# Attention by pairs of heads in plain fp32, on halves of the TensorE array, in a two-layer hybrid decoder

## The chip, the core and the metric

The kernel runs on one core of one Trainium2 chip. The metric is device time in microseconds (us) from launch to end; lower is better. The engines are TensorE (PE in the profile, PEld for its weight loads), VectorE (DVE), ScalarE (ACT), GpSimd (POOL) and SyncE (SP), which here issues most DMAs.

## The reference

Two layers over 512 tokens of width 1024. Each layer first mixes the tokens by three groups that read slices of one input projection, then runs a gated feed-forward net (FFN) of width 2816 with a short convolution. All data are float32.

```python
for l in range(DEPTH):
    h = rms_norm(x, attn_norm[l])
    (q_a, k_c, v_c, k_s, v_s, k_w, v_w, gate_a,
     c_q, c_kv, k_r, u) = jnp.split(h @ w_in[l], split_points, axis=-1)
    o_a = nsa_attention(...)
    o_b = mla_attention(...)
    o_c = s5_ssm(...)
    mix = jnp.concatenate([rms_norm(o_a, ...), rms_norm(o_b, ...), rms_norm(o_c, ...)], axis=-1)
    x = x + mix @ w_out[l]
    x = x + conv_ffn(rms_norm(x, ffn_norm[l]), ...)
return rms_norm(x, final_norm)
```

The two attention groups have six heads each. In the first, "NSA", a head has 64 query columns, three heads share one key and value head, and each head is attended three times: over 31 compressed blocks, over selected blocks (with 512 tokens all of them are selected, so this is plain causal attention) and over a window (again causal). The three results are added with gates. In the second, "MLA", a head has 96 query columns (64 plus 32 rotary ones), and one causal attention. So a layer has 6 x 2 + 6 = 18 causal attentions of 512 x 512 with 64 value columns.

## The kernel before, in words

**Numbers.** TensorE takes a float32 operand in two ways here. Plain `F32` is the ordinary one. `F32R` is a rounded form. The kernel gets float32 accuracy from the rounded form by splitting an operand into a rounded high part and a remainder: `split` writes the high part with ACT and the remainder with DVE or POOL. A product is then two or three matmuls, high x high, high x low, low x high (`mm3`, L239 to L242). Nearly all matmuls of the kernel are of this kind; each works on the full 128 x 128 array.

**A head.** One head is one unit (MLA) or two (NSA: selected, window). A unit has four stages. Stage 0 prepares operands. For NSA, `prep` stacks the high part of the 64 query rows on their remainder, 128 rows in all, and the high key part twice (L1038 to L1056), so that two matmuls of 128 rows make the scores. For MLA, `proj_q` projects 128 query rows (L928 to L943) and the scores are three matmuls. Stage 1, `head_scores` (L511), makes four blocks of scores, 128, 256, 384 and 512 columns wide, because the attention is causal; DVE adds the mask and takes the row minimum (L520), ACT takes the exponential with the row sum (L523). Stage 2, `head_scale` (L526), multiplies by the reciprocal sum and the gate on POOL (L532). Stage 3, `head_pv` (L539), does for each of four key blocks j: 4 - j transposes of 128 x 128 on PE (L544), a split of the transposed block from PSUM (ACT the high part, DVE the remainder, L546), and two matmuls (L548). Their weights are the high and the low value part side by side, 64 + 64 columns, so the head's result is the sum of two halves of the output, which `out_evac` (L570) adds with ACT and DVE. For NSA, two more matmuls (L1076) add the compressed attention.

**Order.** `pipeline` (L554) runs the units with the stages shifted by one unit each, in the order 2, 1, 3, 0. The other work of the mixer (projections, the state-space group, norms, the first part of the output projection) hangs on steps of this pipeline by the tables `PLAN0` and `PLAN1`, one for each layer. The framework then schedules the instructions with its own estimate of times, so what stands on an engine is not the order of the source; each engine runs its instructions in the order that results.

**Memory.** PSUM's eight banks are dealt out by name: two for projections ("mm", "kq"), two for scores ("s"), two for transposes ("t"), one for the result of a head ("o"), and one for everything small ("x"). SBUF has 128 x 512 tiles `f` (float32) and pairs of such tiles `r` (rounded: high and low).

**Norms.** `rstd_` (L248) computes a norm's factors for 512 tokens as 4 columns and spreads each over 128 rows by a matmul with the identity (L271).

## Time and profile before

| | |
|---|---|
| median of 3 runs | 1374.46 us (1372.62 to 1374.56) |
| span of the profiled execution (first to last instruction) | 1372.3 us |
| PE, PEld busy share of the span | 95%, 79% |
| DVE, ACT, POOL busy share | 62%, 47%, 53% |
| PE in the chain that ended last | 72% |

The profile has no end-to-end time of its own execution beside the span; the median run is 2.2 us longer than that span, so a change of the span is taken as a change of the time. In the tables of the profile, "bank" is a PSUM bank, "wt" a weight tile after its split, "raw" one before it, "sml" a small column tile, "cst" the constants (mask, identity). A plain fp32 matmul of the program stands in the trace as two MATMUL records; an F32R matmul and a transpose stand as one. Busy time of PE overlaps between neighbours, since a matmul's record reaches from its start to the end of its pipeline.

### The profile page before, as it was taken

What the parts mean: (1) busy time and instruction counts of PE and PEld (TensorE: products, weight loads), DVE (VectorE), ACT (ScalarE), POOL (GpSimd) and SP (SyncE); (2) the same over time, 40 slices, a digit from 0 to 9 for tenths busy, and PEclk for the clock granted to TensorE, in tenths of its full rate; (3) what the DMA queues carried; (4) which work ended last, traced back from release to release, by engine and by line L of the source; (5) the groups of instructions that cost most, each with busy time, mean ns of one, the idle gap of its engine ahead of it and who ended that gap; (6) DMA issues with size and microseconds to landing.
All of it is one profiled execution on the core that took longest, in us unless ns stands there. A gap on an engine that the chain in (4) does not pass through costs nothing.

```text
span 1372.3 us, 19205 instructions
## 1 busy us (share of the span) xinstructions
PE 1302.4 (95%) x6414; PEld 1079.2 (79%) x6414; DVE 856.5 (62%) x1733; ACT 638.8 (47%) x1322; POOL 724.4 (53%) x722
## 2 busy tenths in 40 slices
PE   7888989998998999999999999999999999999997
PEld 5676777786876888888888887877878888888886
DVE  6988889858695334643466488986764433442455
ACT  4334667754443233423443356886453323332344
POOL 7485546654759155545437665556376315612532
PEclk9989999999999999999999999999999999999998
DMA  6243622212333333443353433121223333333332
GB/s 224 83 131 99 182 85 66 68 62 64 98 99 113 111 95 100 117 124 95 112 173 112 149 124 106 59 60 43 83 85 106 95 100 99 94 92 106 95 94 83
DMA packets 91556, 140.14 MB, mean 102 GB/s; under 512 B 15553, under 2 KB 36545, under 8 KB 91457
## 3 DMA queue, kind: packets, MB, share of 16 engines
q1 hardware_dynamic: 90176, 134.72, 32.2%
q0 software_dynamic: 1280, 4.20, 1.0%
q8 instruction: 50, 0.82, 0.3%
q14 instruction: 50, 0.40, 0.1%
HBM read 125.01 MB, written 15.96 MB: 103 GB/s over the span
## 4 chain that ended last, share of the span: by engine, by line
PE 72%; DVE 19%; issue 3%; POOL 2%; ACT 2%; DMA 2%; SPq 0%; DVEq 0%; POOLq 0%; ACTq 0%
PE bank L240 21%; PE bank L241 20%; PE bank L242 20%; DVE r L227 3%; PE bank L519 2%; PE bank L548 2%; DVE f L520 2%; PE bank L544 2%; DVE r L230 1%; DVE f L304 1%; DVE f L1157 1%; PE bank L271 1%; PE bank L816 1%; PE bank L253 1%; POOL wt L227 1%
## 5 line engine op out<-in xcount | busy, mean ns | idle before, releaser
L240 PE MATMUL bank<-r,wt 128*128 128x512 f32 x1466 | 580.9, 397 | 15.2 <-ACT wt L226 7.3
L241 PE MATMUL bank<-r,wt 128*128 128x512 f32 x1466 | 577.0, 394 | 4.4 <-DVE r L230 3.6
L242 PE MATMUL bank<-r,wt 128*128 128x512 f32 x1466 | 573.4, 394 | 5.1 <-POOL wt L227 5.1
L227 POOL TENSOR_TENSOR wt<-raw,wt 128x512 fp32r<-128x512 f32 (+2 forms) x272 | 355.0, 1309 | 300.1 <-ACT wt L226 291.0
L226 ACT CAST wt<-raw 128x512 fp32r<-128x512 f32 (+2 forms) x398 | 231.0, 584 | 332.5 <-PE bank L241 189.6
L240 PEld LDWEIGHTS bank<-r,wt 128*128 128x128 f32 x1466 | 278.2, 190 | 77.2 <-ACT wt L226 8.9
L242 PEld LDWEIGHTS bank<-r,wt 128*128 128x128 f32 x1466 | 278.0, 190 | 66.1 <-POOL wt L227 8.5
L241 PEld LDWEIGHTS bank<-r,wt 128*128 128x128 f32 x1466 | 278.4, 190 | 62.8 <-DVE r L230 6.5
L227 DVE TENSOR_TENSOR wt<-raw,wt 128x512 fp32r<-128x512 f32 (+3 forms) x126 | 88.9, 709 | 51.7 <-ACT wt L226 51.3
L294 POOL TENSOR_TENSOR f<-f,f 128x512 f32<-128x512 f32 (+1 forms) x53 | 68.0, 1284 | 99.9 <-ACT f L286 98.4
L532 POOL TENSOR_SCALAR f<-f,sml 128x128 f32<-128x128 f32 (+3 forms) x144 | 79.3, 569 | 52.2 <-DVE sml L530 18.0
L227 DVE TENSOR_TENSOR r<-bank,r 128x256 fp32r<-128x256 f32 (+4 forms) x196 | 90.2, 476 | 24.2 <-ACT r L226 23.0
L1182 DVE TENSOR_TENSOR f<-bank,f 128x512 f32<-128x512 f32 x44 | 30.3, 690 | 112.6 <-PE bank L242 103.1
L1188 POOL TENSOR_TENSOR f<-f,f 128x512 f32<-128x512 f32 x44 | 58.0, 1320 | 74.6 <-ACT f L1187 74.6
L523 ACT ACTIVATE f<-f,sml 128x384 f32<-128x384 f32 (+3 forms) x144 | 80.6, 560 | 32.5 <-DVE sml L520 31.6
L226 ACT CAST r<-bank 128x256 fp32r<-128x256 f32 (+4 forms) x196 | 79.0, 417 | 31.8 <-PE bank L544 15.7
L548 PE MATMUL bank<-r,r 128*128 128x512 f32 (+3 forms) x288 | 82.1, 353 | 10.4 <-DVE r L227 7.5
L519 PE MATMUL bank<-r,r 128*128 128x128 f32 (+3 forms) x336 | 79.3, 339 | 9.8 <-DVE sml L520 9.5
L226 ACT CAST r<-f 128x512 fp32r<-128x512 f32 (+1 forms) x76 | 46.9, 620 | 80.5 <-DVE f L1189 65.7
L520 DVE CUSTOM_DVE_ANT_0 f<-bank,cst 128x384 f32<-128x384 f32 (+3 forms) x144 | 67.8, 481 | 12.7 <-PE bank L519 11.6
L1189 DVE TENSOR_TENSOR f<-bank,f 128x512 f32<-128x512 f32 x44 | 30.4, 690 | 72.7 <-POOL f L1188 68.9
L1217 DVE TENSOR_TENSOR f<-bank,f 128x512 f32<-128x512 f32 x48 | 32.7, 688 | 65.6 <-PE bank L242 65.5
(225 smaller groups left out, 1549.9 us busy)
## 6 DMA issues: line engine op xcount, KB each, us to landing
raw<-in_wup_dram SPq DMA_DIRECT2D x176, 256.0 KB
raw<-in_wdn_dram SPq DMA_DIRECT2D x72, 256.0 KB
raw<-in_win_dram SPq DMA_DIRECT2D x64, 256.0 KB
f<-pd SPq DMA_DIRECT2D x32, 256.0 KB
raw<-in_wout_dram SPq DMA_DIRECT2D x32, 192.0 KB
f<-in_xT_dram SPq DMA_DIRECT2D x16, 256.0 KB
f<-in_w_dram SPq DMA_DIRECT2D x16, 256.0 KB
pd<-f SPq DMA_DIRECT2D x16, 256.0 KB
```

The source lines that it names most:

```text
L226: A.copy(hi, src)
L227: (E or V).tensor_tensor(lo, src, f32(hi), op=OP.subtract)
L240: PE.matmul(p, lhsT=w[:, 0, o:o + n], rhs=x[:, 0], start=start, stop=False)
L241: PE.matmul(p, lhsT=w[:, 0, o:o + n], rhs=x[:, 1], start=False, stop=False)
L242: PE.matmul(p, lhsT=w[:, 1, o:o + n], rhs=x[:, 0], start=False, stop=stop)
L294: G.tensor_tensor(a, a, q, op=OP.add)
L519: PE.matmul(p[:, :w], lhsT=q[:, i * 128:w], rhs=k[:, :w], start=n == 0, stop=n == len(passes) - 1)
L520: V.tensor_tensor_reduce(out=sm[i], in0=p[:, :w], in1=C("mask")[:, 512 - w:], op0=OP.add, op1=OP.min, scale=1.0, scalar=3.0e38, accum_out= ...
L523: A.activation(sm[i], sm[i], AF.Exp, bias=mx[:, i:i + 1], scale=-1.0, accum_out=su[:, i:i + 1])
L532: G.tensor_scalar(sm[i], sm[i], rs[:, i:i + 1], 1.0, op0=OP.mult, op1=OP.mult)
L548: PE.matmul(o[:, j * 128:], lhsT=v[j], rhs=pr[:, x, :w], start=first and j == 0 and x == 0, stop=last and j == 3 and x == 1)
L1188: G.tensor_tensor(t, t, r_f, op=OP.mult)
```

## The change

Two heads make one unit, nothing in attention is split any more, and its operands are plain fp32.

- **Scores** (`pair_scores`). NSA: the two heads' queries lie in rows 0 to 63 and 64 to 127 of one tile, their keys likewise, and each head's block is one matmul of 64 rows, on the upper or the lower half of the array, into a bank of its own. The heads are permuted on the host so that head m and head m + 3 share a tile. MLA: one matmul of 128 rows for each head and block, on the full array.
- **Values** (`pair_pv`). The transposed blocks are copied from PSUM once (in turn by ACT and DVE, `pcopy="AVAVA"`, five copies of 512 columns for a pair) and used whole. Each head's matmul has 64 weight columns: one head writes rows 0 to 63 of the result, the other rows 64 to 127. The result is copied once by ACT; `out_evac` is gone. The compressed attention (L1061 of the changed kernel) is one such matmul for each head.
- **Operands.** Keys, values and rotary parts are copied instead of split; `prep` of NSA is empty.
- **Norm factors** are spread by `PE.transpose` instead of a matmul with the identity.
- **Banks.** "s" has three banks and takes what "x" had; "t" two, "o" one.
- **Plan.** There are nine units for each layer instead of 18, and the steps of the tables are about halved.

```diff
-CFG = dict(plan=(PLAN0, PLAN1), F=dict(main=15, aux=10, side=12), R=dict(main=16, side=3, q=3, pr=2), nraw=3, nw=4, hp=50,
-           order=(2, 1, 3, 0), rings=dict(), tabs=2, lead=(0, 0, 3, 4), units=('NNNNNNMMMMMM', 'NNNNNNMMMMMM'), rest=((-7, -1, -1, -5, -7, -1, -1, -1), (-1, -1, -3, -1, -1, -1, -1, -1)),
+CFG = dict(plan=(PLAN0, PLAN1), F=dict(main=24, aux=10, side=12), R=dict(main=16, side=3), nraw=3, nw=4, hp=50,
+           order=(2, 1, 3, 0), rings=dict(), tabs=2, lead=(0, 0, 3, 4), units=('NNNMMM', 'NNNMMM'), pcopy="AVAVA", rest=((-7, -1, -1, -5, -7, -1, -1, -1), (-1, -1, -3, -1, -1, -1, -1, -1)),
...
-    rings = dict(kq=banks[0:2], mm=banks[0:2], s=banks[2:4], t=banks[4:6], o=banks[6:7], x=banks[7:8], up=banks[0:4], dn=banks[4:8], w2=banks[0:4] + banks[6:8] + banks[2:4])
+    rings = dict(kq=banks[0:2], mm=banks[0:2], s=banks[2:5], t=banks[5:7], o=banks[7:8], up=banks[0:4], dn=banks[4:8], w2=banks[0:4] + banks[6:8] + banks[2:4])
...
     def ps(kind):
+        kind = "s" if kind == "x" else kind
...
-            PE.matmul(p[:, i * 128:(i + 1) * 128], lhsT=y[:, i:i + 1].to_broadcast([128, 128]), rhs=ident, start=True, stop=True)
+            PE.transpose(p[:, i * 128:(i + 1) * 128], y[:, i:i + 1].to_broadcast([128, 128]), ident)
...
-    def head_scores(passes):
-            p = ps("s")
-            for n, (q, k) in enumerate(passes):
-                PE.matmul(p[:, :w], lhsT=q[:, i * 128:w], rhs=k[:, :w], start=n == 0, stop=n == len(passes) - 1)
+    def pair_scores(qk):
+            p = [ps("s"), ps("s")]
+            for x, (q, k) in enumerate(qk):
+                PE.matmul(p[x][:, :w], lhsT=q[:, i * 128:w], rhs=k[:, :w], start=True, stop=True)
...
-    def head_pv(o, b, sm, v, first, last):
-            pr = R.get("pr")
-            split(p[:, :w], pr[:, 0, :w], pr[:, 1, :w])
-            for x in range(2):
-                PE.matmul(o[:, j * 128:], lhsT=v[j], rhs=pr[:, x, :w], start=first and j == 0 and x == 0,
-                          stop=last and j == 3 and x == 1)
+    def pair_pv(o, b, sm, v, first, last):
+        for k, js in enumerate(((0,), (1, 3), (2,))):
+            for n, part in enumerate(todo):
+                p, c = ps("t"), 0
...
+                if cfg["pcopy"][2 * k + n] == "A":
+                    A.copy(t, p)
+                else:
+                    V.tensor_copy(t, p)
...
+            for j in js:
+                for x in range(2):
+                    PE.matmul(o[64 * x:64 * x + 64, j * 128:], lhsT=v(x, j), rhs=pt[x, j], start=first and j == 0, stop=last and j == 2)
...
-    def out_evac(o, dst):
-        t = F.get()
-        A.copy(t[0:64], o[64:128])
-        V.tensor_tensor(dst, o[0:64], t[0:64], op=OP.add)
-        F.free(t)
...
-                for r in range(6):
-                    V.scalar_tensor_tensor(hrep[:, r, 0:31], a[:, c], 1.0, hy[:, c], op0=OP.add, op1=OP.mult)
+                V.scalar_tensor_tensor(hy, a, 1.0, hy, op0=OP.add, op1=OP.mult)
+                for kv2 in range(2):
+                    V.tensor_copy(shp(hr, 4, 2, 32)[:, 0:3, kv2, 0:31],
+                                  hy[:, kv2 * 31:kv2 * 31 + 31][:, None, :].to_broadcast([128, 3, 31]))
...
             def scores():
-                qs, K = qsl[h][:, 0], KS[g, bi]
-                st["s"] = head_scores([(qs, K[:, 0]), (qs, K[:, 1])])
+                q, k = pj[f"q{m}"], pj[("ks", "kw")[bi]]
+                st["s"] = pair_scores([(q[r:r + 64], k[r:r + 64]) for r in (0, 64)])
```

What the scheduler makes of it is seen on PE. The first place is in the second layer, among the NSA units. Before, PE's stream there reads as follows (L519: a score matmul, x2 two of them back to back; L544: a transpose; L548: a value matmul; L500 is the state-space group, L780 MLA's values):

```order
L519 MATMUL bank3_154<-r4_104,r19_119 128x512 x2
L500 MATMUL bank7_158<-f30_93,f29_92 128x64
L548 MATMUL bank6_157<-r22_122,r5_105 128x512
L780 MATMUL bank0_151<-wt3_130,r0_100 128x384
L780 MATMUL bank1_152<-wt3_130,r0_100 128x384
L548 MATMUL bank6_157<-r22_122,r5_105 128x512
L548 MATMUL bank6_157<-r23_123,r5_105 128x384
L544 MATMUL bank4_155<-cst_159,f5_68 128x128
L544 MATMUL bank4_155<-cst_159,f8_71 128x128
```

In the changed kernel the same stretch reads so (L527: a score matmul on a row half; L576: a value matmul on a column half; L564: a transpose on the full array):

```order
L527 MATMUL bank3_158<-f0_63,f6_69 128x128
L576 MATMUL bank7_162<-f16_79,f33_96 64x384
L576 MATMUL bank7_162<-f11_74,f33_96 64x128
L576 MATMUL bank7_162<-f16_79,f33_96 64x128
L564 MATMUL bank5_160<-cst_163,f28_91 128x128
L564 MATMUL bank5_160<-cst_163,f12_75 128x128
L564 MATMUL bank5_160<-cst_163,f28_91 128x128
L564 MATMUL bank5_160<-cst_163,f29_92 128x128
L527 MATMUL bank3_158<-f0_63,f6_69 128x384
L564 MATMUL bank5_160<-cst_163,f12_75 128x128
L564 MATMUL bank5_160<-cst_163,f28_91 128x128
L564 MATMUL bank5_160<-cst_163,f29_92 128x128 x2
```

Two matmuls of the same 128-row form have become matmuls of single halves, and the partners of a score pair are apart: between one half's matmul and the next stand transposes or value matmuls of another form.

The second place is DVE, also in the second layer's NSA units. Before, it reads so (L227: the remainder of a split, here of a transposed block; L520: mask and minimum of a score block, an ISA row and one that reads its minimum; L479 to L490: the state-space group):

```order
L227 TENSOR_TENSOR r22_122<-bank5_156,r22_122 128x512
L488 TENSOR_TENSOR f31_94<-f31_94 128x256
L227 TENSOR_TENSOR r23_123<-bank4_155,r23_123 128x384
L490 SCALAR_TENSOR_TENSOR f32_95<-r81_3524,f31_94 128x64 x4
L520 ISA f8_71,sml12_143<-bank2_153,cst_159 128x384
L520 ISA sml12_143 128x1
L479 TENSOR_TENSOR f31_94<-f32_95,f27_90 64x4x63 x2
L520 ISA f10_73,sml12_143<-bank3_154,cst_159 128x512
L520 ISA sml12_143 128x1
```

Afterwards (L529: mask and minimum; L570: DVE's copy of a transposed bank; L713, L228, L893 and L231: projections, a weight split, and the state-space group's output):

```order
L529 ISA f23_86,sml2_137<-bank3_158,cst_163 128x384
L529 ISA sml2_137 128x1
L570 COPY f5_68<-bank5_160 128x512
L893 SCALAR_TENSOR_TENSOR f35_98<-f38_101,f35_98 128x512
L539 RECIPROCAL sml8_143<-sml3_138 128x8
L541 TENSOR_TENSOR sml8_143<-sml8_143,gates_171 128x8
L228 TENSOR_TENSOR wt2_133<-raw1_129,wt2_133 128x384
L713 TENSOR_TENSOR f10_73<-bank1_156,f11_74 128x512
L231 SCALAR_TENSOR_TENSOR r17_126<-f35_98,r17_126 128x512
L529 ISA f8_71,sml9_144<-bank2_157,cst_163 128x512
```

The remainders of transposed blocks are gone from DVE, and two of a pair's five plain copies stand there instead.

## Rows read from the trace of the kernel before

**Rows 1.** Page, chain that ended last, by engine.
```profile
PE 72%; DVE 19%; issue 3%; POOL 2%; ACT 2%; DMA 2%; SPq 0%; DVEq 0%; POOLq 0%; ACTq 0%
```
**Rows 2.** Windows: busy time (x instructions) of each engine, granted clock, by stage.
```profile
core 0: us, PE busy (x) PEld busy (x) DVE busy (x) ACT busy (x) POOL busy (x), PEclk, DMA share, GB/s
0.00:105.00 105.00, 84.94 (x385) 69.08 (x386) 88.32 (x162) 40.48 (x68) 73.79 (x82) 0.93 0.45 145
105.00:313.00 208.00, 190.20 (x1084) 157.96 (x1083) 164.78 (x464) 132.77 (x347) 115.17 (x151) 0.96 0.30 93
...
361.00:719.00 358.00, 352.22 (x1587) 287.84 (x1586) 186.33 (x264) 137.91 (x228) 186.00 (x160) 1.00 0.37 111
...
777.00:965.00 188.00, 177.65 (x1034) 150.57 (x1034) 153.26 (x444) 130.41 (x341) 111.79 (x143) 1.00 0.26 82
```
**Rows 3.** PE timeline, full-array and 16-column matmuls: start us, us, engine line.
```profile
578.44 0.39 PE L240 MATMUL bank<-r,wt 128*128 128x512 f32 x1
578.67 0.39 PE L241 MATMUL bank<-r,wt 128*128 128x512 f32 x1
578.99 0.21 PE L447 MATMUL bank<-f 128*16 128x16 f32 x2
579.05 0.35 PE L448 MATMUL bank<-f,f 128*16 128x112 f32 x2
...
579.78 0.35 PE L448 MATMUL bank<-f,f 128*16 128x112 f32 x2
580.06 0.50 PE L240 MATMUL bank<-r,wt 128*128 128x512 f32 x1
580.40 0.40 PE L241 MATMUL bank<-r,wt 128*128 128x512 f32 x1
```
**Rows 4.** PE timeline: four transposes; the spreading of one norm's factors (eight records).
```profile
568.84 0.60 PE L440 MATMUL bank<-cst,f 128*128 128x128 f32 x4
...
1016.11 1.05 PE L271 MATMUL bank<-cst,sml 128*128 128x128 f32 x8
```
**Rows 5.** Groups by form of PE, 777 to 965 us: busy us, mean ns, idle before.
```profile
L240 PE MATMUL bank<-r,wt 128*128 128x512 f32 x106 | 42.9, 406 | 0.2 <-DVE r L227 0.2
...
L544 PE MATMUL bank<-cst,f 128*128 128x128 f32 x180 | 31.5, 274 | 1.0 <-DVE r L227 1.0
...
L843 PE MATMUL bank<-f,f 128*128 128x64 f32 x4 | 0.6, 260 | 0.0
```
**Rows 6.** Waits of PE's weight loads, 777 to 965 us: total us, times, longest.
```profile
PEld bank L548 <- DVE r L227: 9.5, 13, 1.5
PEld bank L519 <- DVE sml L520: 2.5, 4, 1.2
```
**Rows 7.** Page, groups of the heads' matmuls, whole kernel.
```profile
L548 PE MATMUL bank<-r,r 128*128 128x512 f32 (+3 forms) x288 | 82.1, 353 | 10.4 <-DVE r L227 7.5
L519 PE MATMUL bank<-r,r 128*128 128x128 f32 (+3 forms) x336 | 79.3, 339 | 9.8 <-DVE sml L520 9.5
```
**Rows 8.** PE timeline, one plain fp32 matmul of 512 columns (two records).
```profile
896.20 1.02 PE L764 MATMUL bank<-f,cst 128*128 128x512 f32 x2
```
**Rows 9.** Groups by form of DVE, 777 to 965 us.
```profile
L227 DVE TENSOR_TENSOR r<-bank,r 128x512 fp32r<-128x512 f32 x20 | 13.7, 686 | 5.2 <-ACT r L226 5.1
...
L227 DVE TENSOR_TENSOR r<-bank,r 128x128 fp32r<-128x128 f32 x30 | 8.0, 280 | 2.1 <-ACT r L226 2.1
L573 DVE TENSOR_TENSOR f<-bank,f 64x512 f32<-64x512 f32 x11 | 7.5, 682 | 1.1 <-ACT f L572 0.9
```
**Rows 10.** Chain that ended last, first layer's start: start us, us, what.
```profile
68.26 1.66 DVE r L1055
...
94.41 3.95 DVE f L841 x6
...
103.54 2.71 DVE f L850 x5
...
128.50 3.78 DVE r L1055
```

More of the change, by code (lines that the diff above doesn't have):

```diff
@@ L768, in k_rope @@
                 r0 = 64 if b == 0 else 0
-                KF.append(R.get())
-                split(p[r0:r0 + 64], KF[b][r0:r0 + 64, 0], KF[b][r0:r0 + 64, 1])
+                KF.append(F.get())
+                A.copy(KF[b][r0:r0 + 64], p[r0:r0 + 64])
         def mla_v():
             uv = wload(wuv[l], 384)
-            mv.extend(R.get() for _ in range(3))
+            mv.extend(F.get() for _ in range(4))
             for i in range(4):
@@ L956, in pv @@
-                if b == 0:
-                    ob.append(F.get())
-                out_evac(o, ob[m][64 * b:64 * b + 64])
-                if b == 1 and late == "M":
+                pair_pv(o, *st["s"][:2], lambda x, j: mv[j][:, (2 * m + x) * 64:(2 * m + x) * 64 + 64], True, True)
+                t = F.get()
+                A.copy(t, o)
+                ob.append(t)
+                if late == "M":
                     join(ob[m], 3 + m)
@@ L1019, in nsa_v @@
                 PE.transpose(p[:, i * 128:(i + 1) * 128], pj[n][:, i * 128:(i + 1) * 128], ident)
-            p4 = shp(p, 4, 2, 64)
-            for g in range(2):
-                v = vsv(g)[:, bi]
-                split(p4[:, :, g, :], v[:, :, 0, :], v[:, :, 1, :])
+            vs[bi] = F.get()
+            A.copy(vs[bi], p)
             F.free(pj[n])
-        def vsv(g):
-            return vs[g][:, :, :].rearrange("p s (i x d) -> p s i x d", i=4, x=2)
         oa = []
-        KS, qsl, ops = {}, {}, {}
@@ L1069, in pv @@
             def pv():
                 if bi == 0:
-                    ops[h] = ps("o")
-                head_pv(ops[h], *st["s"][:2], [vsv(g)[:, bi, j].rearrange("p x d -> p (x d)") for j in range(4)],
-                        bi == 0, False)
+                    ops[m] = ps("o")
+                pair_pv(ops[m], *st["s"][:2], lambda x, j: vs[bi][:, j * 128 + x * 64:j * 128 + x * 64 + 64], bi == 0, False)
                 if bi == 1:
                     for x in range(2):
-                        PE.matmul(ops[h], lhsT=vc[:, h].rearrange("p a b -> p (a b)"), rhs=pct[h // 4][:, x],
-                                  start=False, stop=x == 1)
-                    if b == 0:
-                        oa.append(F.get())
-                    out_evac(ops[h], oa[m][q0:q0 + 64])
-                    if b == 1 and late == "N":
+                        h = 2 * m + x
+                        PE.matmul(ops[m][64 * x:64 * x + 64], lhsT=vc[:, h], rhs=pct[h // 4], start=False, stop=True)
+                    t = F.get()
+                    A.copy(t, ops[m])
+                    oa.append(t)
+                    if late == "N":
@@ L1136, in tile_trunk @@
                 end.setdefault(t, []).append(tasks[n])
-        heads = dict(N=iter([[nsa_unit(h, bi) for bi in range(2)] for h in range(6)]),
-                     M=iter([[mla_unit(m, b)] for m in range(3) for b in range(2)]))
+        heads = dict(N=iter([[nsa_unit(m, bi) for bi in range(2)] for m in range(3)]),
+                     M=iter([[mla_unit(m)] for m in range(3)]))
         pipeline([u for g in order for u in next(heads[g])], mid, end)
@@ L1288, in _lay @@
     put("cvb2", a["nsa_cv_b2"][None])
[L1289 removed]
+    put("gateb", a["nsa_gate_b"][None][:, :, gp])
     put("are", np.concatenate([a["ssm_a_re"].transpose(2, 0, 1)] * 2, 0))
```

196 lines of the change are left out of this document (92 added, 104 removed), and 12 rows, old and new, of tables (PLAN0, PLAN1).

## The prediction

> **What bounds the kernel now.** I read the chain by engine first: 72% of it is PE and 19% DVE [rows 1]. So PE sets the time where it has enough work, and DVE some of the rest. Then the windows [rows 2]. In the FFN (361 to 719 us) PE is busy 352 of 358 us, and the change touches nothing there. The attention heads lie in 105 to 313 us (first layer) and 777 to 965 us (second): 208 + 188 = 396 us, with PE busy 190.2 and 177.7. Only 28 us are idle, but busy time counts the pipeline behind every matmul that had to wait. What PE must issue comes from start-to-start times. Neighbouring 512-column F32R matmuls start 0.23 us apart (578.44, 578.67), though one lasts 0.39 [rows 3]; I use 0.227, which is 0.443 ns a column. Four transposes span 0.60 us, the last of them 0.27 long, so 0.11 each [rows 4, 5]. With such prices the 26 forms of the second window, 1034 records [rows 2, 5], need about 166 us of its 188, and the first window also about 166 of 208. **PE has 332 us of own work in 396 us; 64 us are gaps.** Where they come from is in the waits: the longest total before PE's weight loads is for the remainders of split blocks (DVE L227), 9.5 us, then the masked scores, 2.5 us [rows 6]. DVE is busy 165 of 208 and 153 of 188 us there, ACT 133 and 130 [rows 2]. So the heads are bound by PE, with gaps that DVE causes.
>
> **The change part by part.**
>
> *Heads' matmuls on PE.* Gone are the 336 score and 288 value matmuls [rows 7] and 24 for the compressed part, 648 F32R matmuls with 211,968 columns by the code's widths (128 to 512): 211,968 x 0.443 ns = 94 us. New ones are plain fp32. Such a matmul of 512 columns is two records that span 1.02 us [rows 8]. An F32R matmul lasts 0.39 us and holds the array for 0.227 [rows 3], so 0.16 of a span is pipeline behind the work; the two records hold the array for 0.86 us, 0.43 each, nearly four times F32R's. That is 1.67 ns a column. MLA's scores go from three F32R matmuls to one plain one on the full array: 15,360 columns, 25.6 us. The half-array matmuls (96 scores, 156 values, 82,944 columns) cost 138 us if each runs alone. That is 138 + 25.6 - 94 = **+70 us with no overlap**. If every partner ran wholly beside its twin, they would cost 69, and the term would be +1.
>
> Between these bounds the trace has no row, since no matmul of the kernel works on a half beside another. What can overlap I take from the order: matmuls issue in order, so a half runs beside its twin only if they are neighbours. Of the 252 half-array matmuls, 107 stand directly behind one of the other half (85 value matmuls, 22 scores) with 29,824 columns; the scheduler has put transposes or projections between the others, as the two PE pieces of the order show. Each plain matmul is two passes long in two records, A, A', B, B'; of a lone pair A' can run beside B, which saves one record of four. 29,824 x 0.83 ns = 25 us. I take **+45 us**.
>
> *Norm factors.* 60 matmuls (eight records spanning 1.05 us for four of them [rows 4], about 0.11 a record) become transposes of 0.11: **-7 us**.
>
> *Changes of form.* The 16-column matmuls of the state-space group show what it costs when the array goes from one form to another [rows 3]. L241 starts at 578.67 and holds the array for 0.227; the next, of 16 columns, could start at 578.90 and starts at 578.99. On the way back L448's last record starts at about 579.87 (the second of two that start 0.095 apart) and ends its streaming by 579.97; L240 starts at 580.06, and its successor 0.34 later instead of 0.23, as its weights could not be loaded ahead. So about 0.1 us in and 0.2 back before an F32R matmul; before a transpose the same reading gives 0.15. The built order has 16 such changes before, 279 after: 263 more. At 0.145 each, **+38 us**; the bounds are nothing, where PE waits at that moment anyway, and 0.2 each, 53 us.
>
> The trace shows this for a form of 16 columns alone [rows 3]. The Trainium skill ("TensorEngine Tiling (Array Packing)", Key Properties) says that switching between tiling modes, not between tiles of one mode, drains TensorE. By it the halves pay as the 16 columns do, +38; if only the narrow form paid, 0. No run here shows it for halves.
>
> *PE in all:* 45 - 7 + 38 = +76 us.
>
> *DVE, ACT, POOL.* A head's four remainders take DVE 0.69, 0.55, 0.41 and 0.28 us, 1.93 in all (the two between lie on the line of the first and last [rows 9]); 36 heads, 69 us. `out_evac`: 24 x 0.68 = 16 us [rows 9]. New on DVE are 36 copies of 512 columns; at 0.69, the price of the nearest DVE read of a bank [rows 9], 25 us. Net about -60 us of the 318 that DVE is busy in the heads, and ACT and POOL lose some work too. This shortens nothing by itself; it takes gaps out of PE. The waits for L227 go altogether, those for masked scores stay. No DMA is moved.
>
> *Start of the first layer.* There PE has 85 us of work in 105, DVE 88 [rows 2], and the chain runs through instructions that the change takes away or merges: L1055 (1.7 and 3.8 us, stretched), six L841 (4.0), five L850 (2.7) [rows 10]. Of these 12 us perhaps 4 come back as the new copies and products: **-8 us**. What is late next is DVE's state-space work on the same chain.
>
> *Sum.* PE then has 332 + 76 = 408 us of own work for what took 396. So even with no gap left the heads are 12 us longer. Of 64 us of gaps I keep 24: the waits on split blocks go, DVE has a fifth less to do, and PE, now the later one, finds operands ready more often; but masked scores, the fill and the end of a pipeline with units twice as large stay. 408 + 24 - 396 - 8 = +28. The profiled span and the median run are taken to move alike: 1374.5 + 28 = **1402 us**. With no gap left it is 1378; with all 64 left, 1442.
>
> **The rivals.**
>
> *The halves do not overlap at all.* Nothing in the trace shows that they do. Then +70 in place of +45: 1427 us.
>
> *New waits keep the gaps.* "s" has three banks for pairs and for all that used "x", so a score block can wait for a norm or a state-space block, and POOL and ACT take a pair in blocks twice as large. For it speaks that PE's score matmuls wait for DVE already [rows 7]; against it, that DVE loses a fifth of its work. All gaps left: 1442 us.
>
> *Faster: changes of form cost nothing.* If halves switch without a drain, or nearly all changes fall where PE waits for an operand (gaps of 64 us are enough room for 38), PE has 370 us, with 24 of gaps 394, and the start 8 less: 1364 us. It decides from about 0.04 us a change on: 263 x (0.145 - 0.04) is the forecast's 28. Against it: the narrow form pays in the middle of a stream where the neighbours wait for nothing [rows 3].
>
> *Faster: pairs overlap wholly.* For this a half must run beside a twin that stands apart in the order, or all four records of a pair must overlap. Then +1 in place of +45, with the changes of form still paid: 1358 us. The Trainium skill ("TensorEngine Tiling (Array Packing)", Theoretical Speedup) gives up to 2x for a dimension of 64 or less; by it alone the pairs cost this.
>
> **How the numbers follow.** A measurement of this kernel tells 0.2%, 2.7 us, from no change. Chances: the forecast with its own range of 1385 to 1418 us 0.45, no overlap 0.2, gaps kept 0.12, the two faster rivals together 0.19, no change 0.04. So slower 0.77, same 0.04, faster 0.19. The range reaches to the middle of the faster rivals below and to the gaps kept above: 1361 to 1440 us.
>
> **What would show it.** Right, if in the profile after the two score records of a half stand 0.43 us apart at 512 columns, and a change of form leaves 0.09 to 0.2 us between the end of one matmul's streaming and the next; if the heads are longer than 208 and 188 us with PE busier, DVE's busy time falls by some 60 us, and the FFN keeps 358 us. The start would reach the first score matmul some us earlier. Wrong, if neighbours of one form start closer than one record's 0.43 us at many places and the heads are shorter; if PE shows long idle times before L527 with DVE or bank waits behind them (then the banks rule, not PE's work); or if the granted clock of the heads, 0.96 and 1.00 [rows 2], falls, for which I have no term.

## The result, and the profile after

The changed kernel takes 1470.78 us (median of 4 runs, 1470.67 to 1472.54) against 1373.54 for the kernel before beside it: 1.0711 times as long, 95% interval 1.0696 to 1.0726. It is slower, as forecast, but by 97 us in place of 28, and outside the range of 1361 to 1440. The chain that ended last has 78% PE and 11% DVE (72% and 19% in [rows 1]): DVE is off the path to a good part, and PE more than fills its place:

```profile
PE 78%; DVE 11%; POOL 3%; DMA 3%; issue 3%; ACT 1%; SPq 0%; POOLq 0%; DVEq 0%; ACTq 0%
```

Windows of the changed kernel, with the columns of [rows 2]: the start in two pieces, the first layer's heads, FFN and start of the second layer, the second layer's heads.

```profile
0.00:105.00 105.00, 72.95 (x311) 57.78 (x312) 76.36 (x150) 31.50 (x54) 58.21 (x73) 0.85 0.43 137
105.00:131.00 26.00, 25.71 (x156) 20.39 (x154) 14.43 (x30) 8.53 (x16) 17.13 (x21) 1.00 0.49 147
131.00:367.00 236.00, 218.70 (x948) 134.42 (x946) 109.40 (x315) 106.37 (x263) 96.31 (x129) 0.91 0.22 68
416.00:777.00 361.00, 351.86 (x1588) 286.73 (x1587) 187.43 (x264) 137.82 (x229) 186.02 (x160) 1.00 0.38 111
845.00:1063.00 218.00, 206.55 (x947) 128.71 (x945) 107.27 (x315) 105.51 (x261) 94.45 (x127) 0.96 0.22 65
```

The heads take 236 + 218 us in place of 208 + 188 [rows 2]: +58, where the forecast had +36 (+76 of work, 40 of gaps gone). In the first 105 us PE did 311 instructions in place of 385, and the first score comes at 131 us, 26 later; the forecast had it 8 earlier. The granted clock of these 105 us fell too, from 0.93 [rows 2] to 0.85; the lost 0.08 of 105 us is 8 us, the most that it can have cost of the 26. The rest stands before the second layer's heads: from the end of the first layer's to the first score of the second's are 479 us instead of 464, partly work that only changes its place (between the last norm and that score PE has 287 records in 55 us; before, 236 in 44).

So the start is the largest surprise. The longest waits of PE in it, first of the changed kernel (30 to 131 us), then of the kernel before (30 to 105 us): total us, times, longest.

```profile
PE bank L847 <- DVE f L846: 9.8, 1, 9.8
PE bank L241 <- DVE f L713: 4.7, 1, 4.7
PE bank L441 <- DVE f L713: 3.3, 1, 3.3
PE bank L241 <- DVE bd L851: 2.3, 1, 2.3
```

```profile
PE bank L829 <- DVE f L828: 3.6, 1, 3.6
PE bank L816 <- DMA f<-in_w_dram: 2.9, 1, 2.9
PE bank L816 <- DVE bd L834: 2.3, 1, 2.3
```

L847 of after is L829 of before: the compression's second matmul, which needs DVE's GELU. PE's timeline at this place, first after, then before (start us, us, engine, line):

```profile
45.14 3.81 PE L834 MATMUL bank<-f,f 128*128 128x62 f32 x32
58.71 0.69 PE L847 MATMUL bank<-f 128*128 128x62 f32 x2 [9.76 <-DVE f L846]
61.67 0.80 PE L241 MATMUL bank<-r,wt 128*128 128x512 f32 x1 [2.28 <-DVE bd L851]
```

```profile
45.54 3.81 PE L816 MATMUL bank<-f,f 128*128 128x62 f32 x32
49.10 0.48 PE L241 MATMUL bank<-r,wt 128*128 128x512 f32 x1
49.42 0.39 PE L242 MATMUL bank<-r,wt 128*128 128x512 f32 x1
```

Before, projections follow the compression at once, 0.23 us apart, and cover DVE's GELU. After, PE stands 9.8 us and then 2.3 more. What the small blocks had was bank 7, alone; now they take turns in "s", banks 2 to 4, and "up", the ring of these projections, is banks 0 to 3. So a small block can hold a bank that a projection needs; the wait of L241 for L851, which reads the compression's result out of its bank, is of this kind. The experiments test whether that is the cause.

In the heads the halves look like this. PE's timeline in the second layer: L576 and L1061 are column halves, L527 a score matmul (the first row a pair on row halves), L564 transposes, L243 the F32R projection before a lone half; x4 at L1061 is two matmuls of two records each.

```profile
973.07 0.49 PE L527 MATMUL bank<-f,f 64*128 64x128 f32 x4
...
985.66 0.65 PE L576 MATMUL bank<-f,f 128*64 128x256 f32 x4
986.14 1.03 PE L1061 MATMUL bank<-f,vc 128*64 128x512 f32 x4
987.10 0.66 PE L564 MATMUL bank<-cst,f 128*128 128x128 f32 x4
...
1004.99 0.39 PE L243 MATMUL bank<-r,wt 128*128 128x512 f32 x1
1005.31 0.86 PE L576 MATMUL bank<-f,f 128*64 128x384 f32 x2
1006.10 0.66 PE L564 MATMUL bank<-cst,f 128*128 128x128 f32 x4
```

Two neighbouring matmuls of 512 columns on opposite halves span 1.03 us together, what one spans alone on the full array, 1.02 [rows 8]. Each record of one runs beside the same record of the other, so a lone pair saves half of its time, not the quarter of the forecast. Row halves do the same: the pair of 128 columns spans 0.49 us, and a lone half of 128 columns 0.48 (at 219.91 us in the last fence). Yet the heads are longer than forecast. The experiments separate what overlap gives from what the halves cost.

### The profile page after: what moved, and what is told of

Its sections match the earlier page's. It is cut to its first block, busy times and chain, and to the rows that moved or that the text cites. A ratio compares the mean times of both kernels' runs of the same rounds, so it can differ in the third digit from the quotient of the medians.

```text
span 1470.8 us, 18403 instructions
## 1 busy us (share of the span) xinstructions
PE 1382.0 (94%) x6306; PEld 1048.2 (71%) x6306; DVE 752.8 (51%) x1475; ACT 584.7 (40%) x1158; POOL 690.2 (47%) x702
## 4 chain that ended last, share of the span: by engine, by line
PE 78%; DVE 11%; POOL 3%; DMA 3%; issue 3%; ACT 1%; SPq 0%; POOLq 0%; DVEq 0%; ACTq 0%
PE bank L241 20%; PE bank L243 20%; PE bank L242 20%; PE bank L527 6%; PE bank L576 5%; PE bank L564 3%; DVE r L231 1%; PE bank L254 1%; POOL wt L228 1%; DVE f L305 1%; DMA f<-pd 1%; DVE f L1141 1%; PE bank L834 1%; DVE f L529 1%; POOL f L426 0%
## 5 line engine op out<-in xcount | busy, mean ns | idle before, releaser
L241 PE MATMUL bank<-r,wt 128*128 128x512 f32 x1466 | 586.6, 401 | 29.8 <-ACT wt L227 6.8
L243 PE MATMUL bank<-r,wt 128*128 128x512 f32 x1466 | 575.8, 396 | 8.6 <-POOL wt L228 7.9
L228 POOL TENSOR_TENSOR wt<-raw,wt 128x512 fp32r<-128x512 f32 (+2 forms) x272 | 352.4, 1300 | 340.1 <-ACT wt L227 335.5
L227 ACT CAST wt<-raw 128x512 fp32r<-128x512 f32 (+2 forms) x398 | 231.2, 585 | 414.8 <-PE bank L242 236.3
L241 PEld LDWEIGHTS bank<-r,wt 128*128 128x128 f32 x1466 | 279.3, 191 | 106.8 <-issue 10.8
L243 PEld LDWEIGHTS bank<-r,wt 128*128 128x128 f32 x1466 | 279.1, 190 | 74.3 <-POOL wt L228 12.2
L228 DVE TENSOR_TENSOR wt<-raw,wt 128x512 fp32r<-128x512 f32 (+3 forms) x126 | 88.8, 708 | 62.5 <-ACT wt L227 62.2
L527 PE MATMUL bank<-f,f 64*128 64x256 f32 (+7 forms) x288 | 105.7, 506 | 6.7 <-DVE sml L529 4.3
L544 POOL TENSOR_SCALAR f<-f,sml 128x128 f32<-128x128 f32 (+3 forms) x144 | 76.1, 549 | 75.3 <-DVE sml L541 38.4
L529 DVE CUSTOM_DVE_ANT_0 f<-bank,cst 128x512 f32<-128x512 f32 (+3 forms) x144 | 68.8, 489 | 81.5 <-PE bank L527 74.8
L534 ACT ACTIVATE f<-f,sml 128x512 f32<-128x512 f32 (+3 forms) x144 | 80.4, 559 | 70.3 <-DVE sml L529 64.2
L1166 DVE TENSOR_TENSOR f<-bank,f 128x512 f32<-128x512 f32 x44 | 30.4, 690 | 112.2 <-PE bank L243 101.9
L576 PE MATMUL bank<-f,f 128*64 128x256 f32 (+3 forms) x288 | 76.6, 464 | 3.3 <-ACT f L568 3.3
L527 PEld LDWEIGHTS bank<-f,f 64*128 64x128 f32 (+1 forms) x288 | 43.8, 200 | 41.7 <-issue 14.8
L564 PEld LDWEIGHTS bank<-cst,f 128*128 128x128 f32 x360 | 42.2, 147 | 43.8 <-issue 35.7
L231 DVE SCALAR_TENSOR_TENSOR r<-f,smt,r 128x512 fp32r<-128x512 f32 x44 | 52.0, 1191 | 36.9 <-ACT r L230 36.7
L1173 DVE TENSOR_TENSOR f<-bank,f 128x512 f32<-128x512 f32 x44 | 30.4, 690 | 73.3 <-POOL f L1172 70.6
L227 ACT CAST r<-f 128x512 fp32r<-128x512 f32 x56 | 34.6, 622 | 75.4 <-DVE f L1173 64.5
```

The lines of the kernel that those rows point to most:

```text
L227: A.copy(hi, src)
L228: (E or V).tensor_tensor(lo, src, f32(hi), op=OP.subtract)
L241: PE.matmul(p, lhsT=w[:, 0, o:o + n], rhs=x[:, 0], start=start, stop=False)
L243: PE.matmul(p, lhsT=w[:, 1, o:o + n], rhs=x[:, 0], start=False, stop=stop)
L527: PE.matmul(p[x][:, :w], lhsT=q[:, i * 128:w], rhs=k[:, :w], start=True, stop=True)
L529: V.tensor_tensor_reduce(out=sm[x][i], in0=p[x][:, :w], in1=C("mask")[:, 512 - w:], op0=OP.add, op1=OP.min, scale=1.0, scalar=3.0e38, accu ...
```

## The experiments

Times of the kernel before beside the runs lie between 1373.1 and 1374.0 us (medians).

**1. A bank for the small blocks alone.**

```diff
-    rings = dict(..., s=banks[2:5], t=banks[5:7], ...)
+    rings = dict(..., s=banks[2:4], x=banks[4:5], t=banks[5:7], ...)
-        kind = "s" if kind == "x" else kind
```

> The changed kernel with one PSUM bank given back to the small blocks: "x" has bank 4 for itself again and "s" the two banks 2 and 3, as many as before the change. The changed kernel takes 1470.8 us; its first score comes at 131 us (before: 105.5) and its second layer's heads start at 845.6 (before: 777). Theory A, the shared banks: the norms and state-space blocks that were on a bank of their own now stand in the ring of the scores, which lies on banks of the first projections, and hold PE up at the start of each layer. Then the first score comes at about 105 to 110 us and the span is 20 to 38 us shorter, 1433 to 1450 us, less what the heads lose by a ring of two banks for pairs. Theory B, the rival: the start is longer because the compression and the norms were merged and reordered, and the banks have no part in it. Then the first score stays at 125 to 135 us and the time within 8 us of 1471, or longer by the heads.

1433.7 us, ratio 1.0438 (1.0420 to 1.0456): 37 us gained, theory A. The first score comes at 103.8 us. PE's timeline at the place shown above:

```profile
46.78 3.61 PE L833 MATMUL bank<-f,f 128*128 128x62 f32 x30
50.13 0.48 PE L241 MATMUL bank<-r,wt 128*128 128x512 f32 x1
50.45 0.39 PE L242 MATMUL bank<-r,wt 128*128 128x512 f32 x1
```

The projections are back behind the compression. So 27 of the 37 us lie before the first score. A ring of two banks for pairs of scores costs the heads nothing in sum (242 + 207 us against 236 + 218).

**2. Everything on the full array.**

```diff
-                    PE.matmul(o[64 * x:64 * x + 64, j * 128:], lhsT=v(x, j), rhs=pt[x, j], ...)
+                    PE.matmul(o[:, j * 128:], lhsT=v(x, j), rhs=pt[x, j], ...)   # v(x, j): 128 columns
...
-                st["s"] = pair_scores([(q[r:r + 64], k[r:r + 64]) for r in (0, 64)])
+                st["s"] = pair_scores([(q, k), (q, k)])
```

> The changed kernel with every half-array matmul made a matmul on the full array, with the same columns: scores use all 128 rows (both heads' queries and keys together) and values all 128 columns (both heads' values, both heads added into one result), so the attention result is another one. No form of the array changes in the heads (22 changes in the program in place of 279), and no two matmuls can run beside each other. The changed kernel takes 1470.8 us. By the terms of the prediction the overlap of neighbours saves 25 us and the changes of form cost 38, so this kernel should be 13 us faster, 1458. Theory A, from the trace after: neighbours overlap wholly, in 29,824 columns at 1.67 ns, so the overlap is worth 50 us, and the changes cost about 25: this kernel is about 25 us slower, 1496. Theory B: changes of form, the weight loads that cannot go ahead over them and the lower granted clock cost more than any overlap gives: this kernel is 15 us faster or more, below 1456, and its granted clock in the heads is above 0.95.

1445.5 us, ratio 1.0528 (1.0515 to 1.0542): 25 us faster than the changed kernel, theory B. So what the halves cost is more than what their overlap gives, by 25 us; by the terms of the prediction it was 13. Its windows of the heads:

```profile
131.00:349.50 218.50, 202.32 (x944) 148.27 (x942) 109.08 (x315) 105.87 (x263) 96.17 (x129) 0.96 0.24 73
828.00:1036.00 208.00, 198.59 (x947) 144.30 (x945) 105.73 (x314) 105.49 (x261) 94.80 (x127) 0.99 0.22 68
```

The granted clock is 0.96 and 0.99, where the halves have 0.91 and 0.96.

**3. Scores alone, values alone, on the full array.** The edits of experiment 2, one at a time.

> The changed kernel with its NSA scores alone on the full array (both heads' 64 rows together, so the scores are others), values still on column halves: 164 changes of form in place of 279, and 85 of the 107 neighbouring pairs kept, with 22,528 of 29,824 columns. With all of them on the full array the kernel is 25.3 us faster than the changed one (1445.5 against 1470.8). If a change of form costs c and a neighbouring column saves y, then 257 c - 29,824 y = 25. Theory A, the price of the prediction, c = 0.145 us, so y = 0.41 ns: 115 c - 7,296 y = 14 us faster than 1470.8, 1457. Theory B, neighbours overlap wholly, y = 1.67 ns, so c = 0.29 us with everything that a change brings (a weight load that cannot go ahead, a lower clock): 21 us faster, 1450.

1451.4 us, ratio 1.0565 (1.0544 to 1.0586): 19 us faster.

> The changed kernel with its values alone on the full array (both heads' 64 weight columns together, both heads added into one result), scores still on row halves: 148 changes of form in place of 279, and 22 neighbouring pairs with 6,656 columns left of 107 with 29,824. By the two theories of the run with full scores: A, a change 0.145 us and a neighbouring column 0.41 ns: 131 x 0.145 - 23,168 x 0.00041 = 9.5 us faster than 1470.8, 1461. B, a change 0.29 and a column 1.67 ns: 38 - 38.7, no faster than the changed kernel, 1471.

1464.4 us, ratio 1.0660 (1.0641 to 1.0678): 6 us faster. The two add up to the 25 of experiment 2. Both lie between the theories; solved together the two equations give 1.06 ns for a neighbouring column and 0.24 us for a change of form with all that it brings. Two equations fix two prices without testing them; experiments 4 and 6 do. The row halves, of which 22 of 96 have a neighbour, cost most; the column halves, 85 of 156, nearly pay for themselves.

**4. Both heads on the same half.** The forms and their changes stay, overlap goes.

```diff
+                    PE.matmul(o[0:64, j * 128:], lhsT=v(x, j), rhs=pt[x, j], ...)
+                st["s"] = pair_scores([(q[0:64], k[0:64])] * 2)
```

> The changed kernel with both heads of a pair on the same half of the array: NSA scores both on rows 0 to 63, values both into rows 0 to 63 of the result, which ACT then copies twice (so the second head's attention is lost and the sum stands in both halves). The forms and their changes stay (283 in place of 279), but no matmul can run beside another. So it measures what overlap gives by itself. The changed kernel takes 1470.8 us, the one on the full array 1445.5. By the terms of the prediction overlap gives 25 us: 1496. By the two runs with scores or values alone on the full array it gives 1.06 ns a neighbouring column, 32 us: 1502. If neighbours overlap wholly and all of it counts, 50 us: 1521. Rival: what is saved by overlap is lost again in waits and in a lower granted clock, then within 10 us of 1471, with a higher granted clock in the heads than 0.91 and 0.96.

1489.9 us, ratio 1.0849 (1.0836 to 1.0863): 19 us slower than the changed kernel. So overlap gives 19 us, a little under the forecast's 25 and well under the 32 by the 1.06 ns of experiment 3. Changes of form with what they bring (here also ACT's second copy of each result) cost 1489.9 - 1445.5 = 44 us, more than the forecast's 38; over 261 changes that is 0.17 us each, not 0.24. So the two prices of experiment 3 do not carry over. The windows of the heads, and the same four records as above, now on one half:

```profile
131.00:376.00 245.00, 230.97 (x953) 140.36 (x952) 109.67 (x315) 109.31 (x269) 94.87 (x129) 0.92 0.22 66
854.00:1083.00 229.00, 221.80 (x947) 137.30 (x946) 103.95 (x315) 109.51 (x267) 94.67 (x127) 0.96 0.19 62
```

```profile
1028.92 1.88 PE L1062 MATMUL bank<-f,vc 128*64 128x512 f32 x4
```

1.88 us in place of 1.03: at the array overlap is nearly whole, in the kernel it gives 19 us of the 50 that 29,824 columns at 1.67 ns would make.

**5. Pairs kept together.**

```diff
+                if x == 0:
+                    behind(mm, reader.get(id(p[1])))    # scores: also wait for the other bank's reader
...
+                    if x == 0:
+                        behind(mm, last_copy)           # values: also wait for the later copy
```

> The changed kernel with its pairs kept together: the first half's matmul of a pair also waits for what the second's waits for (the same bank's reader for scores, the later copy for values), so that the scheduler puts the two behind each other. 50,176 half-array columns then stand directly behind one of the other half (29,824 in the changed kernel), and there are 189 changes of form in place of 279. Theory A, neighbours overlap wholly and a change costs 0.1: 20,352 columns at 1.67 ns are 34 us less of PE's work, half of each pair 17 to 34 us, and 90 changes 9 us; less what the first half waits longer: 15 to 40 us faster than 1470.8, 1430 to 1456. Theory B, the waits rule the heads and PE's work does not: a first half that waits for its twin's operand adds waits, within 8 us of 1471 or slower.

1473.9 us, ratio 1.0731 (1.0715 to 1.0748): nothing gained, theory B. Its first layer's heads, and the longest of PE's waits there:

```profile
131.00:367.00 236.00, 203.84 (x952) 131.90 (x950) 109.73 (x317) 107.31 (x264) 95.97 (x129) 0.87 0.22 69
```

```profile
PE bank L535 <- DVE sml L539: 9.4, 15, 0.8
```

PE is busy 204 us in place of 219, and the window is as long as before: 15 waits of scores (L535) for the mask and minimum of an older block (L539) take the place of the work, and the granted clock falls to 0.87. In the changed kernel the scores wait 2.1 us for such minima in this window.

**6. A bank alone, and pairs kept together for values only.** Experiments 1 and 5 without the wait on scores.

> The changed kernel with a bank for the small blocks alone (1433.7 us by itself) and with the two heads' value matmuls kept together (the first also waits for the second's copy; score matmuls are left alone). 44,800 half-array columns then stand behind one of the other half (33,152 without), and 218 changes of form in place of 268. By 1.06 ns a column and 0.24 us a change, 12 + 12 us faster than 1433.7: 1410. Rival, by the run with scores and values kept together, where more overlap gave nothing: what PE saves goes into waits for the later copy and into a lower granted clock: 1426 to 1440.

1419.7 us, ratio 1.0332 (1.0296 to 1.0369): 14 us gained on 1433.7, between the full price's 24 and the rival's 8 at most; the four runs spread from 1410 to 1425 us, so the size is uncertain. That the wait for a later copy costs less than the wait for a bank is likely, but not shown alone: experiment 5 shared the small blocks' bank, this one does not.

**7. A bank alone and the full array.** Experiments 1 and 2 together.

> Two edits together: a bank for the small blocks alone (37 us faster than the changed kernel by itself, 1433.7) and every half-array matmul on the full array (25 us faster by itself, 1445.5; the attention result is another one). If they cost in different places, the start and the heads, they add up: 1470.8 - 37 - 25 = 1408 us, with the first score at about 104 us and the granted clock of the heads above 0.95. Rival: both give back the same lost time (PE's waits that let the granted clock fall), then 1420 to 1434.

1412.0 us, ratio 1.0279 (1.0262 to 1.0295). They add up, to 59 of 62 us. The first score comes at 103.3 us; the heads:

```profile
103.00:326.00 223.00, 209.22 (x1029) 152.04 (x1028) 121.83 (x347) 110.76 (x273) 107.25 (x144) 0.98 0.28 86
802.00:1003.00 201.00, 195.56 (x947) 144.16 (x946) 104.94 (x318) 105.66 (x263) 95.48 (x129) 1.00 0.23 71
```

**8. Full-array scores with both heads kept apart.** Experiment 6, with keys padded by zeros.

```diff
+                if m == 0:
+                    k = pj[("ks", "kw")[bi]]
+                    kz[bi] = F.get()
+                    G.memset(kz[bi][0:64], 0.0)
+                    A.copy(kz[bi][64:128], k[64:128])
+                    G.memset(k[64:128], 0.0)
-                st["s"] = pair_scores([(q[r:r + 64], k[r:r + 64]) for r in (0, 64)])
+                st["s"] = pair_scores([(q, k), (q, kz[bi])])
```

> The changed kernel with a bank for the small blocks alone and the value matmuls kept in pairs (1419.7 us by themselves), and the NSA scores on the full array with nothing lost: each head's keys stand in a tile whose other 64 rows are zero, so that both heads' queries can be the weights. 104 changes of form in place of 218, 34,304 neighbouring columns in place of 44,800; it costs two more zeroed halves and a copy of 64 rows for each key tile, four in all. Theory, halves of rows cost more in changes than their overlap gives, as in the run with scores alone on the full array (19 us): 1400 to 1408 us. Rival: with pairs kept together and a bank of its own the row halves no longer cost anything: 1415 to 1425.

1404.3 us, ratio 1.0222 (1.0202 to 1.0243), inside the theory's 1400 to 1408. It takes back 66 of the 97 us. The granted clock of the heads is 0.97 and 0.98.

**9. Norm factors, alone and taken back.**

```diff
-            PE.matmul(p[:, i * 128:(i + 1) * 128], lhsT=y[:, i:i + 1].to_broadcast([128, 128]), rhs=ident, start=True, stop=True)
+            PE.transpose(p[:, i * 128:(i + 1) * 128], y[:, i:i + 1].to_broadcast([128, 128]), ident)
```

> The kernel before with one part of the change alone: the norm factors are spread by transposes in place of plain fp32 matmuls with the identity. 60 matmuls of two records each become 60 transposes of one. By the prediction's term PE does 7 us less, 1366.5 us. Rival: these matmuls stand where PE waits for the norm anyway, so that only the last of each group is on the path, 0.1 to 0.5 us for each of 14 norms: 1370 to 1374.

1380.5 us, ratio 1.0052 (1.0038 to 1.0066): 7 us slower, against both expectations. The first score comes at 111.1 us instead of 105.5, and the chain that ended last holds there (start us, us, what):

```profile
83.24 0.69 DVE f L689
...
85.64 6.96 DVE r L1047
92.62 0.69 DVE f L689
```

One subtraction of 64 x 512, L1047, lasts 6.96 us, which in the kernel before lasts 0.69. POOL's timeline at that time shows nine instructions without a pause that end 0.17 us after it:

```profile
85.28 1.44 POOL L227 TENSOR_TENSOR r<-f,r 64x512 fp32r<-64x512 f32 x1
86.69 1.26 POOL L227 TENSOR_TENSOR wt<-raw,wt 128x512 fp32r<-128x512 f32 x1
...
90.78 1.26 POOL L227 TENSOR_TENSOR wt<-raw,wt 128x512 fp32r<-128x512 f32 x1
92.01 0.76 POOL L415 TENSOR_TENSOR f<-f 128x64 f32<-128x64 f32 x1
```

The Trainium skill ("SBUF — State Buffer", Who interferes with whom) says that a DVE instruction with two SBUF inputs contends with a GpSimd instruction that reads SBUF, as an exclusive lock. The rows agree for this one instruction: it starts 0.36 us after POOL's first and ends only as POOL's row does. In the kernel before it came 0.05 us ahead of a POOL row that had no pause either, and did not wait:

```profile
84.73 0.69 DVE L1047 TENSOR_TENSOR r<-f,r 64x512 fp32r<-64x512 f32 x1 [0.16 <-ACT r L226]
```

```profile
84.78 1.77 POOL L227 TENSOR_TENSOR r<-f,r 64x512 fp32r<-64x512 f32 x1 [0.49 <-ACT r L226]
```

So the transposes brought the loss by the order and the moment that they gave these two engines; that PE's own work has no part in it is argued, and the last run below bears it out. Why it waited out the whole row stays open: L310 at 83.85 us, also with two SBUF inputs and beside POOL, took 1.29 us.

> The changed kernel with its norm factors spread by plain fp32 matmuls with the identity again, the rest as it is: 120 records in place of 60 transposes. If the term of the sum holds: 7 us slower than 1470.8, 1478. Rival, the loss seen on the kernel before belongs to the transposes: 5 to 10 us faster, 1461 to 1466.

1477.1 us, ratio 1.0740 (1.0716 to 1.0765): 6 us slower without the transposes, as the term of the sum has it, though this interval and that of the changed kernel overlap.

> The kernel before with one instruction moved off DVE: the second copy of an NSA key remainder is not subtracted once more by DVE but copied by ACT from the remainder that POOL wrote (the same values; four such instructions in each layer). Reference for the run with transposes as well. In the trace of before these subtractions last 0.69 to 1.8 us, 3.1 in all at the start; ACT has room there (40 us of 105). 1369 to 1374 us; if ACT's copy, which waits for POOL, comes later than the subtraction did: to 1380.

1375.8 us, ratio 1.0021 (1.0009 to 1.0033): 2 us slower than the kernel before, above the main range and within that for a late copy.

> The same with norm factors spread by transposes. Theory A, the loss of 7 us by transposes was the one subtraction of 6.96 us beside POOL, which is no longer on DVE: 3 to 7 us faster than the run without transposes. Theory B, the transposes bring it whatever lies on DVE: 5 to 10 us slower than that run.

1373.5 us, ratio 0.9997 (0.9984 to 1.0010): 2.3 us faster than without transposes, theory A in its direction and less in size, and the two intervals touch. With that subtraction off DVE the loss of 7 us is gone. The edit by itself (a copy on ACT in place of `V.tensor_tensor(kk[d0:d0 + 64, 1], ...)`) costs 2 us.

**10. Merged products, alone and with transposes.**

```diff
-                for r in range(6):
-                    V.scalar_tensor_tensor(hrep[:, r, 0:31], a[:, c], 1.0, hy[:, c], op0=OP.add, op1=OP.mult)
+                V.scalar_tensor_tensor(hy, a, 1.0, hy, op0=OP.add, op1=OP.mult)
+                for kv2 in range(2):
+                    V.tensor_copy(hrep[:, 3 * kv2:3 * kv2 + 3, 0:31], ...)
```

> The kernel before with one part of the change alone: the compression's six products on DVE become one product and two copies with repeated operands, and six masked value products become two. In the trace of before the two groups lie on the chain of the first layer's start with 4.0 and 2.7 us. Theory A, the prediction's: about 4 us of these come back, 1369 us, the first score at 101 to 102 us in place of 105.5. Rival: these DVE instructions lasted long because POOL worked beside them, and the wait goes to the next DVE instruction that runs beside POOL: 1372 to 1375 us.

1370.4 us, ratio 0.9980 (0.9968 to 0.9992): 3 us faster than the kernel before, and the only version here that beats both kernels. But the first score still comes at 105.6 us. DVE's timeline where six L841 lasted 3.95 us [rows 10]:

```profile
94.55 0.21 DVE L839 SCALAR_TENSOR_TENSOR f<-f 128x62 f32<-128x62 f32 x1
94.80 0.45 DVE L841 COPY f<-f 128x93 f32<-128x93 f32 x2
96.55 1.31 DVE L426 TENSOR_TENSOR f<-f,ais 128x512 f32<-128x512 f32 x1 [1.30 <-POOL f L415]
97.89 1.65 DVE L427 TENSOR_TENSOR f<-f,f 128x512 f32<-128x512 f32 x1
```

3.95 us have become 0.66. Then DVE waits 1.30 us for POOL, and the next instructions beside POOL last 1.31 and 1.65 us, which lasted 0.68 and 0.69 in the kernel before. The wait went on to them, as the rival had it; the gain came later, in the first layer's heads, which end at 309 us instead of 313.

> The kernel before with two parts of the change: the merged products of the compression (1370.4 us by themselves) and norm factors spread by transposes (1380.5 by themselves). Theory A: the transposes do save PE work, and what they lost alone was one DVE subtraction of 6.96 us that happened to lie beside an unbroken row of POOL instructions at the start; in another order it falls away: 1361 to 1368 us, with the first score at 105 us or before. Theory B: the transposes bring the loss whatever the order: 1374 to 1381.

1380.3 us, ratio 1.0054 (1.0039 to 1.0069): theory B. The subtraction of 6.97 us is there again, at 85.7 us: the merged work comes after it, so the order around it is the same. So theory A's other order was not tested; the subtraction falls away only in the last run of experiment 9, where ACT does its work.

## Why the prediction was wrong, point by point

Four of the kernels form a ladder that adds up to the whole change: before 1373.4, bank alone and full array 1412.0 (+38.6), banks shared 1445.5 (+33.5), halves without overlap 1489.9 (+44.4), halves with it 1470.8 (-19.1). The forecast's terms for these four steps are +15, 0, +38 and -25, so the miss of 69 us is 23.6 + 33.5 + 6.4 + 5.9.

- **Sharing banks: the step that failed.** The forecast put the new sharing of banks at nothing, and gave the start 8 us less. The rival "new waits keep the gaps" named the banks, but put the waits at the scores, in the heads; PE's scores wait there only 2 us in each layer. The waits came in the start, where the small blocks' ring lies on the banks of the first projections: 33 to 37 us by the two pairs of runs that differ in this alone, 27 of them before the first score. It makes about half of the miss.
- **Plain fp32 on the full array, gaps and start.** By the terms 70 - 7 - 40 - 8 = +15; measured +38.6 (experiment 7). The work term is taken to hold, as no run measures it by itself: the forecast's 332 + 70 - 7 = 395 us of own work stands in 223 + 201 = 424 us of heads, and some 10 us of mixer work have gone ahead of the second layer's. That leaves about 40 us of gaps (an estimate from these numbers), not the 24 kept: **gaps were mis-sized**, by some 15 us. DVE's relief was even larger than forecast, 109 + 107 us busy against 165 + 153 [rows 2], 101 less instead of 60, and still did not take the gaps out. The start gives 2 us, not 8: merging DVE's work alone left the first score where it was (experiment 10).
- **Changes of form.** Forecast +38, measured 44 with all that they bring. The prices read from a 16-column form [rows 3] hold for the lone column half at 1005.31 us above: it starts 0.32 us after the F32R matmul ahead of it instead of 0.23; its 768 columns at 0.83 ns take 0.64, and the transposes start 0.79 after it; these four span 0.66 instead of 0.60 [rows 4]. That is 0.30 us for two changes, 0.15 each, and 261 x 0.15 = 39 us of the 44 (an estimate from one place). The Trainium skill ("TensorEngine Tiling (Array Packing)", Key Properties) says that a switch of mode drains TensorE, and the sign of the runs agrees, with 0.17 us a change (44.4 / 261), the lower granted clock included. The faster rival, that changes cost nothing, falls.
- **Overlap.** Forecast -25, measured -19. The mechanism was read wrongly in both directions: neighbours overlap nearly wholly (1.03 us for two matmuls), twice what the step assumed, but of the 50 us only 19 reach the end. Experiment 5 shows where saved work can go: waits for operands and a lower clock, with the window no shorter. The Trainium skill ("TensorEngine Tiling (Array Packing)", Theoretical Speedup) gives up to 2x for a dimension of 64 or less; the single pair comes near it (1.88 against 1.03 us), the kernel does not.
- **Norm factors.** -7 forecast, +6 us when taken back: the changed kernel agrees with it, within noise. Alone on the kernel before it is +7, by one DVE instruction that waits beside POOL.
- **The granted clock**, for which the prediction had no term, fell in the heads from 0.96 and 1.00 to 0.91 and 0.96. What it costs in the heads is contained in the 44 of the changes: by the shares of the windows 245 x 0.08 + 229 x 0.04 = 29 us of clock are lost in experiment 4 (both heads on one half), and 218.5 x 0.04 + 208 x 0.01 = 11 in experiment 2 (full array), so lost clock explains at most 18 of the 44. In the longest low stretch of the changed kernel the clock is at 1.2 GHz throughout, as the first row (a window) shows. PE's timeline below it begins ahead of the fall: lone row halves between transposes, then a wait of 1.89 us for a minimum. In the stretch a lone score half of 512 columns spans 2.07 us, and F32R matmuls of 512 columns stand 0.43 us apart, at the upper level 0.23:

```profile
223.50:257.50 34.00, 26.25 (x64) 14.49 (x64) 11.92 (x40) 14.06 (x34) 13.21 (x17) 0.50 0.18 52
```

```profile
219.91 0.48 PE L527 MATMUL bank<-f,f 64*128 64x128 f32 x2
220.33 0.50 PE L564 MATMUL bank<-cst,f 128*128 128x128 f32 x2
...
221.89 0.57 PE L564 MATMUL bank<-cst,f 128*128 128x128 f32 x2
224.35 2.07 PE L527 MATMUL bank<-f,f 64*128 64x512 f32 x2 [1.89 <-DVE sml L529]
...
255.05 0.63 PE L241 MATMUL bank<-r,wt 128*128 128x512 f32 x1
255.48 0.63 PE L242 MATMUL bank<-r,wt 128*128 128x512 f32 x1
```

- **What held.** Slower; the FFN nearly unchanged (PE busy 352 us in both, 361 us against 358); DVE's fall, which was larger than forecast; waits for split blocks gone, those for masked scores left.

Open stays why the gaps survive although DVE has a third less to do; the runs show only that shorter PE work turns into waits for masks and minima (experiment 5). Untested is whether the gaps come with units twice as large, which every run here keeps. How much of the 44 us is drain and how much clock is known by the two estimates alone, 39 and at most 18, which overlap.

## What to carry to other kernels

When a change merges two rings of buffers, look at every stage that uses their banks, not only at the stage that the change is about: here a bank saved in the heads stopped the projections at the program's start, and cost a third of the loss. Halves of the array save time only where the partners stand next to each other (1.03 against 1.88 us); a change of form cost 0.17 us here, more than a transpose of 128 columns, so halves that are scattered among full-array work lose, and zero-padded operands on the full array were faster (1404 against 1420 us). An engine that loses a third of its work does not hand that time to the bound engine: price the gap by what is waited for, one wait at a time.

## What was not expected of the hardware

- Two neighbouring plain fp32 matmuls on opposite column halves span 1.03 us, one alone on the full array 1.02, both on the same half 1.88.
- The granted clock of the first layer's heads went with the forms: 0.96 on the full array, 0.91 with halves, 0.92 with halves that never overlap, 0.87 with pairs forced together.
- One DVE subtraction of 64 x 512 took 6.96 us in place of 0.69 beside nine POOL instructions without a pause, in two kernels at the same place; where it started 0.05 us ahead of such a row it took 0.69.
